# The output projection's first 1024 columns for the forgetting heads as seven block products, issued among the second half of the stick-breaking heads

## The chip, the cores and the metric

The kernel runs on one core of one Trainium2 chip. The metric is the time on the device in microseconds; smaller is better. Three runs of the kernel before took 1096.7 to 1097.93 us, with a median of 1096.99 us.

## What is computed

One layer on 256 tokens of width 2048, in float32. Eight forgetting heads (softmax with a cumulative forget gate) and eight stick-breaking heads, each 128 wide, read one projection of the normed input. Their outputs are normed by group, and one output matrix brings them back:

```python
merged = jnp.concatenate([rms_norm(from_heads(out_a), out_norm_fox_l),
                          rms_norm(from_heads(out_b), out_norm_sb_l)], axis=-1)
return merged @ w_out_l
...
x = x + hybrid_mixer(h, ...)
h = rms_norm(x, ffn_norm[layer])
x = x + conv_ffn(h, w_up[layer], conv_w[layer], conv_b[layer], w_down[layer])
```

`merged @ w_out` is 256 x 2048 times 2048 x 2048. Its first 1024 rows belong to the forgetting heads and the last 1024 to the stick-breaking heads. The change concerns the forgetting heads' rows.

## The kernel before, in words

**Matmuls.** A float32 operand is kept as a rounded high part and a low rest, and a product is made of three matmuls per block of 128 rows: high x high, low x high, high x low. A block of weights of 128 x 2048 numbers (1 MB) is loaded by a DMA of SP's queue into `w_raw` (three buffers). Then it is split (`split`): ACT rounds it into `w_hi` (L231) and DVE subtracts for `w_lo` (L234), with two buffers each. `in_three` (L248 to L259) issues the matmuls with the activations as the stationary operand (L256); `feature_major` issues those with the weights stationary (L282, L288).

**Seven products.** `in_seven` (L609) multiplies a 2 x 2 block matrix of activations (two tiles of 128 tokens, two groups of four heads) by a 2 x 2 block matrix of weights (four 128-row blocks by 512 columns each) with seven block products in place of eight. A block product is 12 matmuls of 512 columns in one PSUM bank. Some take sums of activation blocks (`block_sums`, then the parts of them) and sums of weight blocks: the first is `w_sum` plus `x12` on DVE (L628), the later ones are accumulating DMAs of POOL's queue (L618). After each product DVE adds the bank to the rows of x, scaled (`residual`, L986). It is a generator: each `next` issues one product.

**Stick-breaking heads.** `sb_head` (L923) is a generator of three parts, and `step` advances two heads at a time, so heads 4 and 5 go together, then 6 and 7. Part one is the scores `ps_z` on PE (L925, L562). ACT and DVE then work on them: three activations (L931 to L933), `sp` (L938), a minimum with the mask (L939), a scan `after` (L941), `e` = scores minus scan (L944), an exponential on ACT (L945), and a second minimum with the mask (L947). Part two is the transposes of `e` into `ps_p` on PE (L811), which ACT copies to `w` and `w1` (L814, L815) and DVE completes (L816). Part three is the product with the values, `ps_o` (L795, L796). ACT takes it out (L396), DVE makes the low part (L397), and ACT squares it (L404).

**Order of the work.** The order on PE is the order in which the code issues. On DVE and ACT it is made by a scheduler when the program is built, and each of these engines then takes its instructions strictly in that order. In the stick-breaking half the code does four pairs of `feature_major` products (queries and keys of four heads), then the values (`project`). Then come, for the forgetting rows of `w_out`, columns 0 to 511 and 512 to 1023 as plain products (`token_major`, 48 matmuls each), with heads 4 to 7 stepped between, and then columns 1024 to 2047 in seven products between the plain products of the stick-breaking rows. After each 512 finished columns `next_rows` transposes x for the next stage: two times four transposes `ps_x` (L149), taken out by ACT (L154) and DVE (L157).

**PSUM.** Each of the pools `psa`, `psb` and `pss` has two buffers. The seven products' `bank_a` and `bank_c` lie in `pss` and `bank_b` in `psb`. The `ps_x` tiles lie in `psb`, the `ps_z` and `ps_p` tiles in `pss`, and `ps_o` in `psb`.

Of the kernel before, what the change touches and what calls it, by code (L numbers as in the profile page):

```python
# [9 lines left out]
F32 = mybir.dt.float32  # L10
# [5 lines left out]
P = 128  # L16
D = 2048
# [29 lines left out]
def hybrid_layer(  # L47
# [251 lines left out]
    def feature_major(w, c0, pool, tag):  # L299

        acc = pool.tile([P, 2, 512], F32, name="pu", tag=tag)
        for kh in range(2):
            from_features(acc, weights(rows_of(w, 8 * kh, 8, c0, 2 * P), 8, 2 * P, 16), kh, low_first=kh == 1)
            step()
        return acc
# [9 lines left out]
    with ExitStack() as actx:  # L315
# [264 lines left out]

        def block_sums(parts):

            blocks = [
                at.tile([P, 4, S], F32, name=f"blocks{h}", tag=tag) for h, tag in enumerate(("minus_c1", "blocks"))
# [17 lines left out]

        def in_seven(src, of_tile, sums, w, x12, add, places, idle_steps, prepared, at_once, cols=512, halfway=None):
# [8 lines left out]
            def of_sums(h, t):  # L612
                return lambda i, part, _: sums[part][:, 4 * h + i, t * P : (t + 1) * P]
# [20 lines left out]
            def product(bank, lhs, parts, to, minus=False):  # L634
                new = bank not in banks
                if new:
                    pool, tag = places[bank]
                    banks[bank] = pool.tile([P, 512], F32, name=bank, tag=tag)[:, :cols]
# [14 lines left out]
            product("bank_a", of_blocks(0, 0), prepared(lambda: split(w, 4, cols), sum_weights), (0, 0))  # L653
            if not at_once:
                yield
                first_loads(moved_x12, (w12,))
# [33 lines left out]
        def values_in_seven():  # L690
# [11 lines left out]
            def prepared(split_first, sum_weights):  # L702
# [5 lines left out]
                lambda i: hT[i], [sums[:, part] for part in range(2)],  # L708
# [80 lines left out]
        def weighted(v, hs, w):  # L789
# [3 lines left out]
            po = psb.tile([P, S], F32, name="ps_o", tag="t")  # L793
# [76 lines left out]
        def sb_heads(c0, scale, parts):  # L870
# [3 lines left out]
            for i in range(0, 4, 2):  # L874
                acc = feature_major(wi, c0 + i * P, psa, "acc")
# [15 lines left out]
        def sb_queries(half):  # L891
# [10 lines left out]
            return sb_heads(B0 + 512 * half, QSCALE, parts)  # L902

        def sb_keys(half):
# [9 lines left out]
            return sb_heads(B0 + WF + 512 * half, 1.0, parts)  # L914
# [6 lines left out]
        def sb_head(h, qT, kT, v):  # L921
            (q0, *q), (k0, *k) = qT[h % 4], kT[h % 4]
# [31 lines left out]
            attended(weighted(v, slice((h % 4) * HD, (h % 4 + 1) * HD), (w, w1)), h, g_sb, 1)  # L954

        for half in range(2):
            qT = sb_queries(half)
            if half:
                fox_sums = block_sums([oT_fox[0][:, 4 * i : 4 * i + 4] for i in range(2)])
            kT = sb_keys(half)  # L960
            v = []
            earlier = list(heads)
            for h in range(4 * half, 4 * half + 4):
                heads.append(sb_head(h, qT, kT, v))
            acc = project(B0 + 2 * WF + 512 * half, 512)

            assert not half or not any(g in heads for g in earlier)
# [4 lines left out]
            values(v, acc)  # L972

# [10 lines left out]
        def residual(t, c, ps, factor):  # L984
            xs = xt[t][:, c : c + 512]
            dve.scalar_tensor_tensor(xs, ps, factor[:, t : t + 1], xs, op0=ALU.mult, op1=ALU.add)  # L986

        def out_in_seven(c0, plus_rg, minus_rg):

            def prepared(split_first, sum_weights):  # L990
                with tc.issue_after(last_head[0].ins), tc.issue_after(last_head[1].ins):
                    parts = split_first()
                    sum_weights()
                    sums.extend(big.tile([P, NH, S], F32R, name="oT_sums", tag=f"hT{g}") for g in (1, 2))
                    block_parts(fox_sums, sums)
                return parts

            def add(t, h, ps, minus=False):
                residual(t, c0 + 512 * h, ps, minus_rg if minus else plus_rg)

            sums = []
            return in_seven(
                [rows_of(wo, 4 * h, 4, c0 + 512 * i, 512) for h in range(2) for i in range(2)],
                lambda i: oT[i], sums, at.tile([P, 2048], F32, name="w_sum", tag="vA"),
                [big.tile([P, 2048], F32, name="x12", tag="hT0")], add,
                {"bank_a": (pss, "s"), "bank_b": (psb, "t"), "bank_c": (pss, "s")}, 3, prepared, True,
            )

        rgs = [const.tile([P, NT], F32, name=f"rg{group}") for group in range(2)]
        minus_rg = const.tile([P, NT], F32, name="minus_rg")  # L1010
        seven = out_in_seven(1024, rgs[0], minus_rg)

        ordered[0] = True
        for group, rg in enumerate(rgs):
            if group == 1:
                finish()
            for c in range(4 if group else 2):
                acc = token_major(
                    lambda k: oT[group * NH + k], wo, group * NH, NH, 512 * c, 512,
                    seven,  # L1020
                )
                if group == c == 0:
                    assert scored[: NH + 4] == list(range(NH + 4))
# [389 lines left out]
```

## Time and profile before

| | |
|---|---|
| median of three runs | 1096.99 us |
| span of the profiled execution | 1094.7 us |
| PE busy | 1089.0 us (99%), 5844 matmuls |
| DVE busy | 907.0 us (83%) |
| ACT busy | 721.8 us (66%) |
| POOL busy | 52.8 us (5%) |
| DMA | 251.15 MB, mean 229 GB/s |

The span is one execution from its first to its last instruction, and it lies 2.3 us under the median of the runs. A row of a group of instructions tells the line, the engine, the operation, output<-inputs by tile name, the shape and the count; then busy time and the mean time of one. A row of the timeline or of the chain tells the start, the time it took, and what ran. In the chain a matmul's time is its share of the pipeline, in the timeline it is the matmul's own time from start to end. PE is TensorE, DVE VectorE, ACT ScalarE, POOL GpSimd, SP the queue that issues most loads.

### The profile page before, as it was taken

What the parts mean: (1) busy time and instruction counts of PE and PEld (TensorE: products, weight loads), DVE (VectorE), ACT (ScalarE), POOL (GpSimd) and SP (SyncE); (2) the same over time, 40 slices, a digit from 0 to 9 for tenths busy, and PEclk for the clock granted to TensorE, in tenths of its full rate; (3) what the DMA queues carried; (4) which work ended last, traced back from release to release, by engine and by line L of the source; (5) the groups of instructions that cost most, each with busy time, mean ns of one, the idle gap of its engine ahead of it and who ended that gap; (6) DMA issues with size and microseconds to landing.
All of it is one profiled execution on the core that took longest, in us unless ns stands there. A gap on an engine that the chain in (4) does not pass through costs nothing.

```text
span 1094.7 us, 14881 instructions
## 1 busy us (share of the span) xinstructions
PE 1089.0 (99%) x5844; PEld 944.8 (86%) x5844; DVE 907.0 (83%) x972; ACT 721.8 (66%) x929; POOL 52.8 (5%) x52
## 2 busy tenths in 40 slices
PE   9999999999999999999999999999999999999998
PEld 7998888888888888888888888888888888888887
DVE  5867878877789776789889988889798889889896
ACT  6756555764665567767767776677676777667753
POOL 0011000000000000001010000100000010100010
PEclk9999999999999999999999999999999999999999
DMA  8697654676639395558999697977979698987985
GB/s 290 228 264 212 215 154 154 195 236 203 214 121 286 114 330 192 178 182 229 281 233 282 193 262 264 258 259 184 324 203 308 206 228 271 258 267 190 323 212 173
DMA packets 182575, 251.15 MB, mean 229 GB/s; under 512 B 4528, under 2 KB 120650, under 8 KB 182250
## 3 DMA queue, kind: packets, MB, share of 16 engines
q1 hardware_dynamic: 162474, 209.67, 58.0%
q0 software_dynamic: 19712, 40.01, 19.7%
q8 instruction: 46, 0.75, 0.3%
q10 hardware_dynamic: 320, 0.53, 0.2%
q14 instruction: 23, 0.19, 0.0%
HBM read 248.08 MB, written 2.11 MB: 229 GB/s over the span
## 4 chain that ended last, share of the span: by engine, by line
PE 99%; DMA 0%; DVE 0%; SPq 0%; issue 0%
PE pu L282 35%; PE acc L256 19%; PE pu L288 18%; PE bank_a L256 12%; PE bank_b L256 6%; PE bank_c L256 3%; PE acc L468 2%; PE acc L1291 1%; PE ps_x L149 1%; PE ps_o L795 1%; PE bank_a L1291 1%; PE ps_p L811 0%; DMA w_raw<-in_w_in_dram 0%; PE ps_o L796 0%; PE ps_h L335 0%; PE ps_s L562 0%
## 5 line engine op out<-in xcount | busy, mean ns | idle before, releaser
L234 DVE TENSOR_TENSOR w_lo<-w_raw,w_hi 128x2048 fp32r<-128x2048 f32 (+1 forms) x192 | 431.8, 2252 | 104.1 <-ACT w_hi L231 103.8
L231 ACT CAST w_hi<-w_raw 128x2048 fp32r<-128x2048 f32 (+1 forms) x192 | 360.9, 1882 | 208.8 <-PE pu L282 58.5
L282 PE MATMUL pu<-hT,w_hi 128*128 128x512 f32 x1664 | 393.9, 390 | 0.0
L282 PEld LDWEIGHTS pu<-hT,w_hi 128*128 128x128 f32 x1664 | 310.4, 188 | 62.9
L288 PEld LDWEIGHTS pu<-hT,w_lo 128*128 128x128 f32 x1664 | 209.0, 189 | 6.8
L288 PE MATMUL pu<-hT,w_lo 128*128 128x256 f32 x1664 | 212.2, 282 | 0.0
L256 PE MATMUL acc<-w_hi,hT 128*128 128x512 f32 (+1 forms) x512 | 113.5, 374 | 0.0
L256 PEld LDWEIGHTS acc<-w_hi,hT 128*128 128x128 f32 x512 | 91.5, 188 | 14.2
L234 DVE TENSOR_TENSOR w_lo<-w_sum,w_hi 128x2048 fp32r<-128x2048 f32 (+1 forms) x38 | 84.2, 2215 | 20.4 <-ACT w_hi L231 20.3
L231 ACT CAST w_hi<-w_sum 128x2048 fp32r<-128x2048 f32 (+1 forms) x38 | 70.3, 1851 | 45.3 <-PE pu L282 35.1
L1108 ACT ACTIVATE tap<-up,ccol 128x256 f32<-128x256 f32 x176 | 74.6, 495 | 0.0
L256 PE MATMUL acc<-w_lo,hT 128*128 128x512 f32 (+1 forms) x256 | 58.9, 372 | 0.0
L1213 POOL DMA_DIRECT2D w_sum<-in_w_down_dram x20 | 25.7, 1283 | 674.6 <-DVE w_lo L234 660.3
L256 PEld LDWEIGHTS acc<-w_lo,hT 128*128 128x128 f32 x256 | 46.4, 188 | 7.5
L256 PE MATMUL bank_a<-w_hi,g 128*128 128x512 f32 x160 | 40.0, 393 | 0.0
L256 PE MATMUL bank_a<-w_hi,s 128*128 128x512 f32 x160 | 40.0, 392 | 0.0
L256 PE MATMUL bank_b<-w_hi,s 128*128 128x512 f32 x160 | 40.0, 392 | 0.0
L256 PEld LDWEIGHTS bank_a<-w_hi,g 128*128 128x128 f32 x160 | 28.9, 189 | 5.3
L256 PEld LDWEIGHTS bank_a<-w_hi,s 128*128 128x128 f32 x160 | 28.9, 189 | 5.2
L256 PEld LDWEIGHTS bank_b<-w_hi,s 128*128 128x128 f32 x160 | 28.9, 189 | 5.2
L1113 DVE TENSOR_TENSOR gate<-gate,tap 128x512 f32<-128x512 f32 x44 | 30.3, 689 | 2.5 <-ACT tap L1108 0.2
L1113 DVE TENSOR_TENSOR val<-val,tap 128x512 f32<-128x512 f32 x44 | 30.3, 689 | 2.3
(282 smaller groups left out, 1165.9 us busy)
## 6 DMA issues: line engine op xcount, KB each, us to landing
w_raw<-in_w_up_dram SPq DMA_DIRECT2D x88, 1024.0 KB, 7.2
w_raw<-in_w_down_dram SPq DMA_DIRECT2D x44, 1024.0 KB, 7.5
w_raw<-in_w_in_dram SPq DMA_DIRECT2D x36, 1024.0 KB, 5.6
w_sum<-in_w_down_dram POOLq DMA_DIRECT2D x20, 1024.0 KB, 9.6
w_raw<-in_w_out_dram SPq DMA_DIRECT2D x14, 1024.0 KB, 5.3
w_raw<-in_w_down_dram POOLq DMA_DIRECT2D x10, 1024.0 KB, 14.7
w_raw<-in_w_in_dram SPq DMA_DIRECT2D x10, 688.0 KB, 4.3
w_raw<-in_w_in_dram SPq DMA_DIRECT2D x6, 512.0 KB, 6.9
```

Source lines behind the costliest of these rows:

```text
L149: nc.tensor.transpose(ps[:, j, t * P : (t + 1) * P], xt[t][:, (k + j) * P : (k + j + 1) * P], ident)
L231: copied = act.copy(hi[:, some], r[:, :m])
L234: rest = dve.tensor_tensor(lo[:, some], r[:, :m], f32(hi[:, some]), op=ALU.subtract)
L256: nc.tensor.matmul(o, lhs(i, l, t), r[:, i, :], start=starts and j == 0, stop=stops and j == 3 * n - 1, skip_group_check=more,)
L282: nc.tensor.matmul(acc[:, j, :], hi[:, i, j * P : (j + 1) * P], hT[k].rearrange("p a b -> p (a b)"), start=k == 0, stop=low_first and k == ...
L288: nc.tensor.matmul(acc[:, j, S:], lo[:, i, j * P : (j + 1) * P], hT[k][:, 0, :], start=False, stop=not low_first and k == KT - 1,)
L468: nc.tensor.matmul(acc[:, t, :], of_half(hT[2 * c + i + j], l, t), r[:, j, :], start=high and c == i == m == 0, stop=not high and c == 7 a ...
L795: nc.tensor.matmul(po, v[j][:, hs], wp[:, k], start=i == 0, stop=False)
L1108: act.activation(taps[w][:, j, :], u[:, j, w : w + S], AF.Copy, scale=ccol[:, w, f : f + 1])
L1113: dve.tensor_tensor(a, a, tap, op=ALU.add)
L1213: nc.gpsimd.dma_start(mem[into][:, : nk * 512].rearrange("p (a b) -> p a b", a=nk), src, accum_op=ALU.add)
L1291: nc.tensor.matmul(o, of_half(g, l, t), r[:, i, c0 : c0 + cols], start=kh == 0 and j == 0, stop=kh == n - 1 and j == 11,)
```

## The change

The forgetting rows of columns 0 to 1023 become a second set of seven products, `first_seven`; those of columns 1024 to 2047 stay in seven, as `second_seven`. The block sums and their parts are made once, earlier, and serve both. Until x is loaded for the residual, the upper half of x's buffer holds two temporary tiles: first the rounded sums, then the weight sum's second operand (`x12`, in two halves). So x is loaded again in two parts (`load_again`).

The second stick-breaking half is put in another order: queries and keys of heads 4 and 5, then the values, then queries and keys of heads 6 and 7. Products of `first_seven` are issued between the pieces of the values and of those queries and keys. Heads 4 and 5 are stepped under the values. Heads 6 and 7 are stepped under two pieces of the stick-breaking rows, the end of `first_seven` and the start of `second_seven`. `ps_o` of heads 4 to 7 moves to `pss`; `bank_a` and `bank_c` move to `psb`, and `bank_b` takes over `bank_c`'s bank.

The core of the diff:

```diff
+                if new and places[bank] in banks:
+                    banks[bank] = banks[places[bank]]
+                elif new:
...
+        def block_parts_in_place(blocks, between, lows):
+
+            for hi, block in zip(between, blocks):
+                in_order(act.copy(hi, block))
+            for h, (hi, block) in enumerate(zip(between, blocks)):
+                for i, n, lo in lows[h]:
+                    in_order(dve.tensor_tensor(lo, block[:, i : i + n], f32(hi[:, i : i + n]), op=ALU.subtract))
+            highs = [at.tile([P, 4, S], F32R, name=f"sum_high{h}", tag=tag) for h, tag in enumerate(BLOCKS)]
+            for high, hi in zip(highs, between):
+                in_order(act.copy(high, f32(hi)))
+            return highs
...
+                {"bank_a": (psb, "t"), "bank_c": (psb, "t"), "bank_b": "bank_c"}, idle_steps, prepared, True,
...
+        qT = queries((0,))
+        fox_blocks = block_sums([oT_fox[0][:, 4 * i : 4 * i + 4] for i in range(2)])
+        group_factors(0)
...
+        kT = keys((0,))
...
+        load_again(0)
...
+        first_seven = out_in_seven(
+            0, at.tile([P, 2048], F32, name="w_sum", tag="vA"), spare, 1, prepared_first
+        )
+        next(first_seven)
...
+        v1, ready = [], []
+        add_heads(4, qT, kT, ready, (pss, "s"))
+        sb_values(1, v1, some_of(".777"))
+        qT = queries((2,), behind=some_of("7."))
+        kT = keys((2,), behind=some_of("7."))
+        ready.extend(v1)
...
+        accs = [new_acc()]
+        out_piece(accs[0], 0, 0)
+        step()
+        next(first_seven)
+        add_heads(6, qT, kT, ready, (pss, "s"))
+        step()
+        assert not next(first_seven, None)
+        load_again(1)
+        accs.append(new_acc())
+        out_piece(accs[1], 1, 0)
+        step()
+        second_seven = out_in_seven(1024, ...)
+        next(second_seven)
+        step()
+        next(second_seven)
+        next(second_seven)
+        finish()
+        next(second_seven)
+        out_piece(accs[0], 0, 4)
+        group_factors(1)
+        completed(0, accs[0])
+        out_piece(accs[1], 1, 4)
+        completed(1, accs[1])
+        waiting.append(next_rows(0))
+        for c in range(2, 4):
+            acc = new_acc()
+            for k in (0, 4):
+                next(second_seven, None)
+                out_piece(acc, c, k)
+                step()
...
```

In the built program PE has 3524 matmuls of 512 columns where it had 3536, and its other matmuls are as before. DVE gets two more operations of 2048 columns, three of 1024 and five of 512 columns. ACT gets two more casts of 2048 and four of 1024 columns. From the first weights of the up-projection on, the order on all engines is as before. Three places show what the new order does; each row has its own kernel's line numbers.

**DVE, heads 4 and 5, from a scan to the second head's masked `e`.** `w_lo` is a weight block's low part, `w<-ps_p` needs the transposes of the head that comes first. Before:

```order
L941 SCALAR_TENSOR_TENSOR after<-go_on,sp 128x384
L944 TENSOR_TENSOR e<-ps_z,after 128x384
L938 SCALAR_TENSOR_TENSOR sp<-ps_z,e 128x384
L947 TENSOR_TENSOR e<-e,masks 128x2x128
L939 TENSOR_TENSOR sp<-sp,masks 128x2x128
L941 SCALAR_TENSOR_TENSOR after<-go_on,sp 128x384
L944 TENSOR_TENSOR e<-ps_z,after 128x384
L234 TENSOR_TENSOR w_lo<-w_raw,w_hi 128x2048
L947 TENSOR_TENSOR e<-e,masks 128x2x128
L234 TENSOR_TENSOR w_lo<-w_raw,w_hi 128x2048
L816 TENSOR_TENSOR w<-ps_p,w 128x256 x2
```

Now:

```order
L956 TENSOR_TENSOR sp<-sp,masks 128x2x128
L987 SCALAR_TENSOR_TENSOR x_2428<-bank_a,rg_1556,x_2428 128x512
L958 SCALAR_TENSOR_TENSOR after<-go_on,sp 128x384
L961 TENSOR_TENSOR e<-ps_z,after 128x384
L234 TENSOR_TENSOR w_lo<-w_raw,w_hi 128x2048
L964 TENSOR_TENSOR e<-e,masks 128x2x128
L955 SCALAR_TENSOR_TENSOR sp<-ps_z,e 128x384
L956 TENSOR_TENSOR sp<-sp,masks 128x2x128
L958 SCALAR_TENSOR_TENSOR after<-go_on,sp 128x384
L833 TENSOR_TENSOR w<-ps_p,w 128x256
L961 TENSOR_TENSOR e<-ps_z,after 128x384
L964 TENSOR_TENSOR e<-e,masks 128x2x128
```

Before, both heads' masked `e` stood ahead of both `w<-ps_p`. Now the first head's `w<-ps_p` stands ahead of the second head's `e` and its mask. On PE the two heads' transposes still follow one another directly.

**DVE, heads 6 and 7, up to the second head's masked `e`.** Before:

```order
L938 SCALAR_TENSOR_TENSOR sp<-ps_z,e 128x384
L405 TENSOR_TENSOR ssq_103<-ssq_103,osq 128x256
L939 TENSOR_TENSOR sp<-sp,masks 128x2x128
L941 SCALAR_TENSOR_TENSOR after<-go_on,sp 128x384
L944 TENSOR_TENSOR e<-ps_z,after 128x384
L938 SCALAR_TENSOR_TENSOR sp<-ps_z,e 128x384
L939 TENSOR_TENSOR sp<-sp,masks 128x2x128
L941 SCALAR_TENSOR_TENSOR after<-go_on,sp 128x384
L944 TENSOR_TENSOR e<-ps_z,after 128x384
L234 TENSOR_TENSOR w_lo<-w_raw,w_hi 128x2048
L947 TENSOR_TENSOR e<-e,masks 128x2x128 x2
```

Now, from the second head's `sp` on:

```order
L955 SCALAR_TENSOR_TENSOR sp<-ps_z,e 128x384
L234 TENSOR_TENSOR w_lo<-w_sum,w_hi 128x2048
L964 TENSOR_TENSOR e<-e,masks 128x2x128
L956 TENSOR_TENSOR sp<-sp,masks 128x2x128
L643 TENSOR_TENSOR w_sum<-w_sum,x_3173 128x2048
L234 TENSOR_TENSOR w_lo<-w_raw,w_hi 128x2048
L234 TENSOR_TENSOR w_lo<-w_sum,w_hi 128x2048
L958 SCALAR_TENSOR_TENSOR after<-go_on,sp 128x384
L987 SCALAR_TENSOR_TENSOR x_2428<-bank_a,rg_1556,x_2428 128x512
L961 TENSOR_TENSOR e<-ps_z,after 128x384
L833 TENSOR_TENSOR w<-ps_p,w 128x256
L964 TENSOR_TENSOR e<-e,masks 128x2x128
```

One operation of 2048 columns stood among the second head's; now there are four.

**PE, where `bank_b` starts.** Before, from the first product in seven on:

```order
L256 MATMUL bank_a<-w_hi,oT_fox 128x512 x8
L256 MATMUL bank_a<-w_lo,oT_fox 128x512 x4
L256 MATMUL bank_c<-w_hi,oT_fox 128x512 x8
L256 MATMUL bank_c<-w_lo,oT_fox 128x512 x4
L256 MATMUL acc<-w_hi,oT_2305 128x512 x8
```

Now, in `second_seven`, where `bank_b` has `bank_c`'s name and place:

```order
L256 MATMUL bank_a<-w_hi,oT_fox 128x512 x8
L256 MATMUL bank_a<-w_lo,oT_fox 128x512 x4
L828 MATMUL ps_p<-cs,e 128x128 x6
L256 MATMUL bank_c<-w_hi,oT_fox 128x512 x8
L256 MATMUL bank_c<-w_lo,oT_fox 128x512 x4
L256 MATMUL bank_c<-w_hi,sum_high_2565 128x512
```

The transposes of heads 6 and 7 stand between `bank_a` and `bank_c`, and `bank_b`'s first product follows `bank_c`'s directly in the same bank, where 24 matmuls stood between.

More of the change, by code (lines that the diff above doesn't have):

```diff
@@ L304, in feature_major @@
             step()
+            next(behind, None)
         return acc
@@ L982, in next_rows @@
             yield
[L984 to L1006, printed above, removed]
-            )
```

166 lines of the change are left out of this document (103 added, 63 removed).

## The prediction

> **What bounds the kernel now.** I read the page first. Its line of busy times has PE at work nearly all the span.
>
> ```profile
> PE 1089.0 (99%) x5844; PEld 944.8 (86%) x5844; DVE 907.0 (83%) x972; ACT 721.8 (66%) x929; POOL 52.8 (5%) x52
> ```
>
> A busy PE need not be a PE at its full pace, so I went on to the chain of waits from 270 to 460 us, the stage of the change. Its columns are start, time and what ran.
>
> ```profile
> 279.86 0.36 PE ps_z L562 x3
> 280.22 10.90 PE acc L256 x48
> 291.12 0.66 PE ps_p L811 x6
> ...
> 326.52 2.72 PE bank_c L256 x12
> ```
>
> The chain there is PE alone, and 48 matmuls of 512 columns in 10.90 us and 12 in 2.72 us are both 0.227 us each: PE runs without a gap, before the seven products and in them. So a matmul less saves 0.227 us, and a wait of PE is lost in full, since nothing later has slack to give it back. The question is how near the other engines are. The timeline of DVE for heads 4 and 5 answers it.
>
> ```profile
> 281.55 0.56 DVE L938 SCALAR_TENSOR_TENSOR sp<-ps_z,e 128x384 f32<-128x384 f32 x1
> 282.14 0.43 DVE L939 TENSOR_TENSOR sp<-sp,masks 128x256 f32<-128x256 f32 x1
> 282.60 0.96 DVE L941 TENSOR_TENSOR_SCAN after<-go_on,sp 128x384 f32<-128x384 f32 x1
> 283.59 0.56 DVE L944 TENSOR_TENSOR e<-ps_z,after 128x384 f32<-128x384 f32 x1
> 284.07 0.55 DVE L938 SCALAR_TENSOR_TENSOR sp<-ps_z,e 128x384 f32<-128x384 f32 x1
> 284.74 0.43 DVE L947 TENSOR_TENSOR e<-e,masks 128x256 f32<-128x256 f32 x1
> 285.08 0.42 DVE L939 TENSOR_TENSOR sp<-sp,masks 128x256 f32<-128x256 f32 x1
> 285.54 0.96 DVE L941 TENSOR_TENSOR_SCAN after<-go_on,sp 128x384 f32<-128x384 f32 x1
> 286.53 0.56 DVE L944 TENSOR_TENSOR e<-ps_z,after 128x384 f32<-128x384 f32 x1
> 287.00 2.28 DVE L234 TENSOR_TENSOR w_lo<-w_raw,w_hi 128x2048 fp32r<-128x2048 f32 x1
> 289.20 0.42 DVE L947 TENSOR_TENSOR e<-e,masks 128x256 f32<-128x256 f32 x1
> ```
>
> The second head's masked `e` is done at 289.62 and PE wants it at 291.12. The margin is 1.5 us: DVE sets no pace, but one split (2.20 from its start to the next row's) more in this piece would.
>
> **The saving.** The first 1024 columns cost two times 48 matmuls and now cost seven times 12. That is 12 fewer, as the counts of the built program say (3536 to 3524), so 12 x 0.227 = 2.7 us. All of it is on the path.
>
> **What DVE is charged.** These rows give the rest of the prices, each from its start to the next where that is shown.
>
> ```profile
> 263.35 0.68 DVE L312 TENSOR_TENSOR t<-pu,t 128x512 f32<-128x512 f32 x1
> 263.95 0.68 DVE L592 TENSOR_TENSOR blocks<-blocks 128x512 f32<-128x512 f32 x1
> ...
> 267.36 0.69 DVE L884 TENSOR_TENSOR k_low<-t,kB 128x512 fp32r<-128x512 f32 x1
> ...
> 321.97 2.29 DVE L628 TENSOR_TENSOR w_sum<-w_sum,x 128x2048 f32<-128x2048 f32 x1
> ...
> 327.17 1.21 DVE L601 TENSOR_TENSOR oT_sums<-blocks,oT_sums 128x1024 fp32r<-128x1024 f32 x1
> 328.30 2.28 DVE L234 TENSOR_TENSOR w_lo<-w_raw,w_hi 128x2048 fp32r<-128x2048 f32 x1
> 334.51 0.74 DVE L986 SCALAR_TENSOR_TENSOR x<-bank_a,rg,x 128x512 f32<-128x512 f32 x1
> ```
>
> A 512-column operation is 0.6, a sum or low part of 1024 columns 1.13, a sum of 2048 columns 2.2 like a split, a residual 0.7. DVE has 2 x 2.2 + 3 x 1.13 + 3 x 0.7 + 2 x 0.6 = 11 us more to do. Spread over the 190 us of that chain, it would fit into its idle time (17% by the page). It isn't spread: the order puts it ahead of what PE waits for. ACT's extra casts are off the path, except as named under C.
>
> **A, the transposes of head 4.** I start at the moment when `k_low` of heads 4 and 5 is ready, which their scores need. From the sum `t` to the end of `k_low` took 4.7 us before (263.35 to 268.05); with ACT's copy ahead of it and four short operations put in, it is near 7, about what PE has from there (`ps_o`, 24 matmuls), so the two come level. From here DVE must do, before head 4's masked `e`: two `ssq` (0.34 each), `sum_low` in three pieces (1.13 + 2 x 0.6), four splits (8.8), the weight sum in two halves (2.26), and head 4's `sp`, minimum, scan, `e` and mask with a residual between (0.5 + 0.46 + 0.99 + 0.48 + 0.42 + 0.7). Sum 17.6. PE has the rest of `ps_z` (0.8) and 60 matmuls (13.6), 14.4. It waits 3.2. If DVE had kept the 1.5 us of margin, 1.7. More, if the weight sum also waits for `x12`:
>
> ```profile
> w_raw<-in_w_in_dram SPq DMA_DIRECT2D x10, 688.0 KB, 4.3
> ```
>
> `x12` takes the place of the rounded sums, so its load goes out only when ACT has copied them. At some 4.3 us for the nearest size, less one split and a piece that DVE does meanwhile, that adds 1.5: the upper end is 4.7.
>
> **B, the transposes of head 5.** This is a closed loop of the new order. PE's transposes of head 4, then ACT's copy, then DVE's `w<-ps_p` of head 4, only then head 5's `e`, its exponential on ACT, its mask, and PE again. The ACT rows:
>
> ```profile
> 287.12 0.53 ACT L945 ACTIVATE e<-e 128x384 f32<-128x384 f32 x1 [0.61 <-DVE e L944]
> ...
> 291.48 0.37 ACT L814 CAST w<-ps_p 128x256 fp32r<-128x256 f32 x1 [0.24 <-PE ps_p L811]
> ...
> 306.49 0.38 ACT L404 ACTIVATE osq<-ps_o 128x256 f32<-128x256 f32 x1
> ...
> 327.47 0.65 ACT L404 ACTIVATE osq<-ps_o 128x256 f32<-128x256 f32 x2
> ```
>
> After head 4's mask DVE has `sp`, minimum and scan of head 5 (1.95, in which PE's three transposes and ACT's copy fit), `w<-ps_p` 0.34, `e` 0.56, the exponential 0.53, the mask 0.42: 3.8, less the 0.33 of the transposes, is 3.5. Were DVE early at A, the first 1.95 would be done, and 0.37 + 0.34 + 0.56 + 0.53 + 0.42 = 2.2 would stay, 2.3 with handovers. It can't be less.
>
> **C, the scores of heads 6 and 7.** `ps_o` of heads 4 and 5 now lies in `pss`, so `ps_z` waits until ACT has squared it. Between the two squares ACT has a cast (1.8). These are the ends of `ps_o` before:
>
> ```profile
> 303.65 0.22 PE ps_o L796 x2
> ...
> 323.55 0.22 PE ps_o L796 x2
> ```
>
> To the last square it took 3.0 us there (303.87 to 306.87) and 4.35 (323.77 to 328.12). PE has 12 matmuls and one head's scores between, 3.3. So 3.0 + 1.8 - 3.3 = 1.5; 0 if the cast falls into ACT's idle time, 2.9 by the slower case.
>
> **D, the transposes of head 7.** From the end of `ps_z` to the second head's `sp` took 3.85 (280.22 to 284.07), at least the 2.5 between the two `sp`, and 4.5 with the residual that stands there now. Then DVE does `sp` 0.5, three splits 6.6, mask and minimum 0.7, the weight sum 2.2, scan 0.99, residual 0.7, `e` 0.56, exponential 0.53, mask 0.42: 13.2. PE has 48 matmuls and three transposes, 11.2. It waits 3.85 + 13.2 - 11.2 = 5.8, between 4.5 and 6.5.
>
> **E and F, PSUM.** For E, `bank_b` can't start before DVE has read `bank_c`. For F, the two `ps_x` tiles of the first `next_rows` share one buffer of `psb`, since `bank_a` of `second_seven` holds the other. The rows, of the chain and then of DVE:
>
> ```profile
> 342.85 2.72 PE bank_b L256 x12
> ...
> 367.84 0.87 PE ps_x L149 x8
> ```
>
> ```profile
> 345.60 0.75 DVE L986 SCALAR_TENSOR_TENSOR x<-bank_b,rg,x 128x512 f32<-128x512 f32 x1 [0.30 <-PE bank_b L256]
> ...
> 368.04 2.29 DVE L234 TENSOR_TENSOR w_lo<-w_raw,w_hi 128x2048 fp32r<-128x2048 f32 x1 [1.87 <-ACT w_hi L231]
> 370.25 1.66 DVE L157 SCALAR_TENSOR_TENSOR hT<-ps_x,pcol,hT 128x256 fp32r<-128x256 f32 x4
> ```
>
> E: the bank ends at 345.57 and the residual at 346.35, so 0.8, taken as 0.9; a second use of the bank may add 1. F: the first tile is read at 371.1, half way through the four, where PE wanted the second at 368.3, so 2.8; without the split ahead 1.8; up to 3.3 if a residual stands there too.
>
> **The sum.** 3.2 + 3.5 + 1.5 + 5.8 + 0.9 + 2.8 = 17.7, less 2.7: 15.0 us. The profiled span of 1094.7 becomes 1109.7, and the median, which is 2.3 above the span, becomes 1112.0. All low ends give 1.7 + 2.3 + 0 + 4.5 + 0.8 + 1.8 - 2.7 = 8.4 (1105.4), all high ones 4.7 + 3.5 + 2.9 + 6.5 + 1.9 + 3.3 - 2.7 = 20.1 (1117.1).
>
> POOL gets accumulating transfers for `first_seven` and x's load in two parts. I cost them at nothing: in the order each lands several pieces of PE work ahead of its reader. If one came late, it would lengthen the waits named.
>
> **The rivals.**
>
> *No waits.* DVE is idle 17% of the span, more than its extra 11 us in the reordered stage. If it ran ahead far enough, PE would keep its pace: 1096.99 - 2.7 = 1094.3, faster. The place is the same DVE queue, and the point is a lead of 3.2 us at `k_low`. Against it: a lead can't open loop B, which PE's own transposes start. Chance 0.04.
>
> *Only the closed loops.* DVE has lead enough for A and C: B 2.3, D 4.5, E 0.8, F 1.8, less 2.7, gives +6.7, 1103.7. The margin of 1.5 speaks against that much lead. Chance 0.12.
>
> *PE slow after long waits.* PE's first matmuls, after idling, ran at half pace; 16 of the same width later took 1.89. The first row is of the timeline, the second of the chain:
>
> ```profile
> 1.06 3.12 PE L421 MATMUL idle<-zeros 128*128 128x256 bf16 x14 [1.06 <-DVE zeros L411]
> ```
>
> ```profile
> 405.69 1.89 PE pu L288 x16
> ```
>
> That is 0.22 against 0.118 each, 1.5 us lost in 3.12. If A with B (6.7 together) and D (5.8) each bring this back, it is 3.0 more: 1115.0. For it, the waits are long; against it, they are broken by three transposes, and no row here shows a wait of such length in mid-run. Chance 0.20. [...]
>
> That the change does not do what it says is out: the counts and the order show it.
>
> **How the numbers follow.** The forecast has 0.62, the rivals 0.04, 0.12 and 0.20, and 0.02 is left for a result near zero. The time is 1112.0. The range reaches from the closed loops alone (1103.7) to the clock case with most of the high ends (20.1 + 3.0 gives 1120.1): 1104 to 1120. About 0.2% (2.2 us) is what a measurement can tell here from no change: faster 0.04, same 0.02, slower 0.94.
>
> **What would show it.** In the profile after, the chain should leave PE for DVE at the transposes of heads 4 to 7, with PE idle before `ps_p` about 3, 3.5 and 6 us, before `bank_b` 1 and before the second `ps_x` 3. If PE's pace stays at 0.227 us through these places, I am wrong about the order's weight; if matmuls after a wait take 0.43 us each, the clock case holds.

## The result and the profile after

The changed kernel takes 1121.21 us (median of four runs, 1118.9 to 1122.6) where the kernel before takes 1096.94 in the same measurement (1096.7 to 1097.93): a ratio of 1.0217, with a 95% interval of 1.0204 to 1.0229. It is slower by 24.3 us. The forecast was slower by 15.0, and its range ended at 1120, 1.2 us below the median.

The busy times on the page of after, to be held against the first line that the prediction shows:

```profile
PE 1096.3 (98%) x5832; PEld 948.0 (85%) x5832; DVE 917.2 (82%) x982; ACT 728.7 (65%) x935; POOL 59.0 (5%) x58
```

PE has 12 matmuls fewer and is busy 7.3 us longer (1096.3 to 1089.0), and the span grew by 25.7 (1120.4 to 1094.7). So there are two losses: PE waits, and what it does takes longer. They separate in the stage from the last transposes of the first half's heads to those of `pcc` in the up-projection, which the windows give as one row for before and one for after; the columns are window, length, then the busy time of PE, PEld, DVE, ACT and POOL, then the granted clock, the DMA share and GB/s.

```profile
243.71:407.42 163.71, 163.60 (x838) 139.43 (x837) 129.67 (x151) 95.63 (x125) 3.90 (x3) 1.00 0.67 207
```

```profile
244.56:433.36 188.80, 169.85 (x823) 142.19 (x822) 139.31 (x158) 102.05 (x129) 10.03 (x9) 0.94 0.71 202
```

The stage is 25.1 us longer. PE idles 18.95 us in it where it idled 0.1, and it is busy 6.25 us more. The mean granted clock fell from 1.00 to 0.94. The idle time is in the list of PE's waits from 240 to 440 us (waiter, what released it, us in total, times, longest); before, that list was empty.

```profile
PE ps_p L828 <- DVE e L964: 13.3, 3, 6.4
PE ps_x L149 <- DVE hT L157: 3.0, 1, 3.0
PE ps_z L942 <- ACT osq L405: 1.8, 2, 1.2
PE bank_c L256 <- DVE x L987: 0.8, 1, 0.8
```

These are A, B and D (first row), F, C and E of the prediction, and no other; in E's row `bank_b` goes by the name of `bank_c`, whose tile it uses. The timeline of PE has each with the work behind it; the bracket is the idle time and its releaser.

```profile
276.47 0.87 PE L828 MATMUL ps_p<-cs,e 128*128 128x128 f32 x3 [4.12 <-DVE e L964]
280.18 0.87 PE L828 MATMUL ps_p<-cs,e 128*128 128x128 f32 x3 [2.84 <-DVE e L964]
280.71 3.76 PE L256 MATMUL bank_c<-w_hi,oT_fox 128*128 128x512 f32 x8
284.27 1.55 PE L256 MATMUL bank_c<-w_lo,oT_fox 128*128 128x512 f32 x4
...
345.27 0.49 PE L828 MATMUL ps_p<-cs,e 128*128 128x128 f32 x3
352.12 0.87 PE L828 MATMUL ps_p<-cs,e 128*128 128x128 f32 x3 [6.36 <-DVE e L964]
...
388.57 1.08 PE L149 MATMUL ps_x<-cs,x 128*128 128x128 f32 x4 [3.00 <-DVE hT L157]
```

The eight first matmuls of the product behind A and B take 3.76 us, 0.45 each from start to start where the prediction reads 0.227, and three transposes take 0.87 where three of the same take 0.49. That is half pace. I laid windows of 3.41 us along the steps in which the granted clock changes (it stands ahead of the DMA share):

```profile
271.60:275.01 3.41, 0.75 (x4) 0.28 (x2) 3.38 (x5) 1.41 (x2) 0.00 (x0) 1.00 1.07 302
275.01:278.42 3.41, 0.87 (x3) 0.50 (x3) 3.34 (x6) 0.54 (x2) 0.00 (x0) 0.50 1.08 271
278.42:281.84 3.42, 1.66 (x6) 1.49 (x7) 1.20 (x4) 1.06 (x3) 0.00 (x0) 0.50 1.07 382
281.84:285.25 3.41, 3.41 (x10) 2.64 (x9) 0.25 (x1) 0.69 (x1) 0.00 (x0) 0.50 0.30 93
...
329.62:333.04 3.42, 2.30 (x12) 1.48 (x10) 3.01 (x5) 1.86 (x2) 0.00 (x0) 1.00 1.03 401
...
346.69:350.10 3.41, 0.00 (x0) 0.00 (x0) 3.41 (x4) 0.34 (x2) 0.81 (x1) 1.00 0.89 136
350.10:353.52 3.42, 1.40 (x5) 1.34 (x6) 1.61 (x4) 1.02 (x3) 0.49 (x1) 0.50 1.09 249
353.52:356.93 3.41, 3.41 (x9) 2.64 (x9) 0.42 (x1) 0.49 (x2) 0.00 (x0) 0.50 1.08 279
...
384.24:387.65 3.41, 1.33 (x8) 0.89 (x7) 2.31 (x2) 1.91 (x3) 0.00 (x0) 1.00 0.06 23
387.65:391.06 3.41, 2.49 (x8) 2.23 (x9) 1.27 (x4) 0.84 (x2) 0.00 (x0) 0.50 0.00 0
391.06:394.48 3.42, 3.42 (x9) 2.64 (x9) 0.38 (x1) 1.38 (x1) 0.00 (x0) 0.50 0.00 0
```

The chain of waits has the twelve products behind D as one piece (start, time, what ran), 4.65 us where twelve took 2.72:

```profile
352.99 4.65 PE bank_c L256 x12
```

A window in which PE had 0.75 us of work is followed by a granted clock of 0.50, and in this run the clock comes back only behind a window that is full (3.41 or 3.42 us). This happens behind A with B (the first four rows), behind D and behind F (the last two groups). It did not happen at C, where PE was busy 2.30 us of a window.

### The profile page after: what moved, and what is told of

The parts are those of the page before. It is cut to its first block, busy times and chain, and to the rows that moved or that the text cites. A ratio compares the mean times of both kernels' runs of the same rounds, so it can differ in the third digit from the quotient of the medians.

```text
span 1120.4 us, 14907 instructions
## 1 busy us (share of the span) xinstructions
PE 1096.3 (98%) x5832; PEld 948.0 (85%) x5832; DVE 917.2 (82%) x982; ACT 728.7 (65%) x935; POOL 59.0 (5%) x58
## 4 chain that ended last, share of the span: by engine, by line
PE 68%; issue 3%; DMA 1%; DVE 1%; ACT 1%; ACTq 0%; POOLq 0%
PE pu L282 29%; PE pu L288 15%; PE bank_a L256 11%; PE bank_b L256 5%; PE bank_c L256 3%; PE acc L256 3%; PE acc L1387 1%; DMA w_sum<-in_w_out_dram 1%; DVE w_lo L234 1%; ACT w_hi L231 1%; PE bank_a L1387 1%; PE ps_x L149 0%; DVE w_sum L643 0%; DVE hT L157 0%; PE ps_p L828 0%
## 5 line engine op out<-in xcount | busy, mean ns | idle before, releaser
L234 DVE TENSOR_TENSOR w_lo<-w_raw,w_hi 128x2048 fp32r<-128x2048 f32 (+1 forms) x190 | 427.2, 2252 | 105.0 <-ACT w_hi L231 104.8
L231 ACT CAST w_hi<-w_raw 128x2048 fp32r<-128x2048 f32 (+1 forms) x190 | 357.1, 1882 | 215.3 <-PE pu L282 61.4
L231 ACT CAST w_hi<-w_sum 128x2048 fp32r<-128x2048 f32 (+1 forms) x42 | 77.8, 1854 | 52.8 <-PE pu L282 35.0
L234 DVE TENSOR_TENSOR w_lo<-w_sum,w_hi 128x2048 fp32r<-128x2048 f32 (+1 forms) x42 | 93.3, 2222 | 19.3 <-ACT w_hi L231 19.3
L1309 POOL DMA_DIRECT2D w_sum<-in_w_down_dram x20 | 25.7, 1284 | 676.8 <-DVE w_lo L234 676.8
```

The lines of the kernel that those rows point to most:

```text
L231: copied = act.copy(hi[:, some], r[:, :m])
L234: rest = dve.tensor_tensor(lo[:, some], r[:, :m], f32(hi[:, some]), op=ALU.subtract)
L1309: nc.gpsimd.dma_start(mem[into][:, : nk * 512].rearrange("p (a b) -> p a b", a=nk), src, accum_op=ALU.add)
```

## The experiments

The theory: PE waits because of the order in DVE's queue (A, B, D), of ACT and DVE steps that stand behind splits (C), and of shared PSUM places (E, F); and these waits take the clock to half behind them. The first rival: the half pace has another cause, or the waits alone explain the time. The second: the load of DVE in this stage counts, not its order. Ratios are to the kernel before.

**1. Filling the waits, in the tile of the transposes.** In `transposed_weights`, and ahead of the second `ps_x`:

```diff
+        def keep_warm(tile, n):
+            for _ in range(n):
+                nc.tensor.matmul(tile, zeros[:, :P], zeros, start=True, stop=True)
...
+            keep_warm(pt[:, 0:2, :].rearrange("p a b -> p (a b)"), warm)
             for i in range(3):
                 nc.tensor.transpose(pt[:, i, :], e[:, i, :], ident)
...
+                if k == 2:
+                    keep_warm(pss.tile([P, S], F32, name="warm", tag="s"), 20)
```

> The changed kernel, with small matmuls on zeros put on PE ahead of the transposes of heads 4, 5 and 7 (30, 18 and 48 of 256 columns, into the tile that the transposes then overwrite) and 20 ahead of the second ps_x, so that PE works through about three quarters of its waits; DVE, ACT and the transfers keep their order. Theory (the waits A to F stay as long as they are, 18.9 us in the profile of after, and the half pace behind them is the rest, 10.0 us): the granted clock shows no half-rate stretch in 265 to 400 us, the products behind the waits take 2.72 us again, and the time falls by 8 to 10 us, to 1111 to 1113. Rival 1 (the half pace comes of the place, not of PE's idleness): the half-rate stretches stay and the time stays within 2 us of 1121. Rival 2 (the waits would be shorter at a full clock, since PE is part of the loop): the time falls by more than 10.

Measured: 1124.01 us, ratio 1.0243 (1.0228 to 1.0259). Neither the theory nor a rival holds: the time rose by 2.8. The reason is the experiment's own. The filling did not start when PE ran dry, since the tile takes the place of `ps_z`, which DVE still reads:

```profile
349.51 7.54 PE L826 MATMUL ps_p<-zeros 128*128 128x256 bf16 x48 [5.25 <-DVE e L966]
```

PE idled 5.25 us at D, the granted clock was 0.50 from 347.08 to 353.90 us, and PE worked through the 48 empty matmuls at half pace for part of the way. The masked `e` was ready at 350.47, and the transposes started at 356.89. At A, B and F the filling left waits of 1.42, 1.27 and 0.81 us, and no half pace stands behind them (granted clock 1.00); but as the filling itself delayed PE, the time of this run does not price the clock.

**2. The heads' steps first.**

```diff
+            with tc.high_priority(offset=2 * AHEAD) if h >= 4 else nullcontext():
                 e = tmp.tile([P, 3, P], F32, name="e", tag="pr")
...
                 dve.tensor_tensor(diagonal, diagonal, limit2, op=ALU.min)
```

> The changed kernel, with the ACT and DVE steps of heads 4 to 7 from Abs to the masked e put ahead of the weight splits in the order; the second head's mask then stands ahead of both w<-ps_p, and only the splits that stand between are behind it. Nothing is left out. Theory (DVE's order makes A, B and D, 13.3 us of waiting, and they bring two of the three half-rate stretches): the waits before ps_p fall to under 3 us together, no half-rate stretch stands behind them, and F with its stretch stays: 1121 less 10 to 13 less about 5 to 6, so 1103 to 1107. Rival (DVE has too much work in this stage, whatever its order): the wait moves from the transposes to the matmuls that need w_lo, PE is idle as long as before and the time stays above 1115.

Measured: 1112.54 us, ratio 1.0141 (1.0124 to 1.0158), four runs from 1109.84 to 1114.58. The list of PE's waits:

```profile
PE ps_p L828 <- DVE e L965: 6.7, 2, 4.5
PE ps_x L149 <- DVE hT L157: 3.0, 1, 3.0
PE ps_z L942 <- ACT osq L405: 2.3, 2, 1.6
PE bank_c L256 <- DVE x L988: 0.8, 1, 0.8
```

The 13.3 us before the transposes became 6.7, in two waits: loop B is open (the second head's mask stands ahead of both `w<-ps_p`), A is halved to 2.2, D fell to 4.5. So order alone was worth 8.7 us of the time. The time lies between the theory (1103 to 1107) and the rival (above 1115): the theory asked for more, but the weight sums and `bank_c`'s split still stood ahead of the second mask.

**3. The second pair of `ps_x` one piece later.**

```diff
             for k in range(4 * c, 4 * c + 4, 2):
                 transposed_split(k, g_ffn)
+                if k == 0:
+                    yield
```

> The changed kernel, with the second pair of the first ps_x tiles one piece of work later, behind the next 12 products and 24 matmuls; the order is otherwise the same. Theory (F is a wait for a PSUM buffer, 3.0 us, and brings the third half-rate stretch, 2.8 us): no wait before ps_x, no half-rate stretch at 385 to 395 us, the time falls by 5 to 6 us, to 1115 to 1116. Rival (the wait is for DVE, which is late anyway): the wait stands before the next bank_a product or the next ps_x instead, and the time falls by less than 2.

Measured: 1115.85 us, ratio 1.0173 (1.0157 to 1.0188), 5.4 less than the change. In its profile no wait stands before `ps_x`, and the granted clock is 1.00 from 356 us on. F cost 3.0 as a wait; the other 2.4 fit the half pace behind it, which is gone too. The theory holds here in both parts.

**4. Both edits.** The built kernel has one thing more than the expectation names: the steps at the end of heads 4 and 5 (the scaled output, its low part, the square and its sum) are put ahead in the order too.

> The changed kernel with both edits: the heads' steps ahead of the splits, and the second pair of ps_x one piece later. Theory: A, B, D and F gone but for 3 us, no half-rate stretch, C 1.8 and E 0.8 left, 12 matmuls fewer (2.7): 1097 + 3 + 2.6 - 2.7, about 1100, between 1097 and 1103. Rival (DVE's work itself is too much, or the late accumulating transfers are the cause): above 1110.

Measured: 1108.03 us, ratio 1.0099 (1.0082 to 1.0116). It lies between the two expectations. PE still waits 2.15 for the transposes of heads 4 and 5, 4.99 before those of head 7, 1.97 at C and 0.84 at E, and behind D the granted clock is 0.50 once more, from 344.81 to 348.22 us. The third edit did not shorten C, which was 1.78 in the changed kernel.

**5. Filling the waits, in the open accumulator.** Zeros added to the sum that PE is in the middle of need no buffer:

```diff
+    def keep_warm(n):
+        for _ in range(n):
+            nc.tensor.matmul(
+                now_open[0][:, 0, :256], idle_zeros[0][:, :P], idle_zeros[0], start=False, stop=False,
+                skip_group_check=True,
+            )
```

> The changed kernel, with PE's waits filled once more, now by matmuls on zeros that add nothing to the accumulator which is open at that place, so that they need no buffer of their own: 30 of 256 columns ahead of the transposes of head 4, 18 of head 5, 46 of head 7 and 20 ahead of the second ps_x. By the first filled run one takes about 0.117 us, so 3.5, 2.1, 5.4 and 2.3 us of waits of 4.1, 2.8, 6.4 and 3.0. Theory (half pace follows PE's idleness): no half-rate stretch, the products behind take 2.72 us, the ends of the waits stay where DVE puts them: 8 to 10 us less, 1111 to 1113. Rival (filling doesn't help, DVE is what counts and the half pace hides in its delays): within 2 us of 1121.

Measured: 1115.21 us, ratio 1.0168 (1.0154 to 1.0183), 6.0 less than the change. Place D in the timeline of PE:

```profile
344.94 0.49 PE L840 MATMUL ps_p<-cs,e 128*128 128x128 f32 x3
345.26 5.18 PE L218 MATMUL acc<-zeros 128*128 128x256 bf16 x46
351.65 0.52 PE L840 MATMUL ps_p<-cs,e 128*128 128x128 f32 x3 [1.20 <-DVE e L976]
```

The transposes of head 7 still start 6.4 us after the wait's beginning, so DVE alone sets that. But they take 0.52 where they took 0.87, and no stretch at half pace is left at A, B, D and F (granted clock 1.00). It is less than the theory asked, and the profiled execution shows why: B is 0.5 longer (PE is sooner where it waits for DVE), C is 2.4 instead of 1.8, and a step at half pace is new at C (0.50 from 331.70 to 335.11 us). That execution is the slowest of the four, 1117.04 us; the others took 1114.98 to 1115.22 at a mean clock of 0.999 to 1.000, so most of them seem to be without this step. PE did nothing useful more and the kernel is 6.0 us faster: at A, B, D and F the half pace went when PE's idleness was filled.

**6. The sums and `bank_c`'s split behind the masks.** On top of the edits of runs 2 and 3, without the third one of run 4 (only the sums of `first_seven` are shown here; those of `second_seven` are gated alike):

```diff
             parts = split_first()
-            sum_weights()
+            with tc.issue_after(masked[-1].ins):
+                sum_weights()
...
-                if here == "7":
+                if here == "m":
+                    last_split.append(masked[-1])
+                if here != ".":
                     next(first_seven)
...
-        next(second_seven)
+        with tc.issue_after(masked[-1].ins):
+            next(second_seven)
```

> The kernel of the last run with both edits, and more of DVE's order: the weight sums of both seven products, and the splits for bank_c, stand behind the second head's masked e, since nothing needs them before. Theory (order alone makes A and D; 2.2 and 5.0 us are left of them in the profile of the kernel with both edits): ps_p waits under 1 us together, a wait before bank_b of 1 to 2.5 may stand in their place, C 2.0 stays: 1098 to 1101. Rival (DVE's load in this stage is what PE waits for, in whatever order): what is moved behind the mask is missing later, PE waits before bank_c and bank_b as long as before ps_p, and the time stays at 1106 or above.

Measured: 1105.23 us, ratio 1.0077 (1.0061 to 1.0093). In its profile no transposes wait any more, and the granted clock is 1.00 all through the stage. This execution is the fastest of the four, 1104.02 us; the others have mean clocks of 0.997 to 0.998 and are 0.7 to 2.4 us longer, so their clock seems to have fallen somewhere. Two waits took the place of those at the transposes, in the first two rows:

```profile
PE bank_c L256 <- DVE x L990: 2.8, 1, 2.8
PE bank_c L256 <- ACT w_hi L231: 2.2, 1, 2.2
PE ps_z L944 <- ACT osq L405: 2.0, 2, 1.6
PE pu L282 <- ACT w_hi L231: 0.8, 1, 0.8
```

The first is a residual behind two splits, before the second `bank_b` product. The second is the weight sum, now too late for `bank_b`. Of 7.1 us of A and D some 5.0 came back elsewhere. Both sides are partly right: order makes the waits at the transposes, and DVE is full enough here that most of what is put first is missing later.

**7. C and E too.** On top of run 6, the splits and casts behind the heads' low parts and squares, and `bank_b` of `second_seven` in `bank_a`'s place. In this kernel `bank_b` overwrites the first product of `bank_a`, to which later products add, so that part of the sums is lost.

```diff
-                {"bank_a": (psb, "t"), "bank_c": (psb, "t"), "bank_b": "bank_c"}, idle_steps, prepared, True,
+                {"bank_a": (psb, "t"), "bank_c": (psb, "t"), "bank_b": again}, idle_steps, prepared, True,
...
+        low_after, cast_after = squared
+        with tc.issue_after(low_after.ins):
             assert not next(first_seven, None)
...
+        with tc.issue_after(cast_after.ins):
             out_piece(accs[1], 1, 0)
```

> The same, with C and E too: the splits and casts that stood between the heads' low parts and squares stand behind them, and bank_b of second_seven takes bank_a's place, which is free by then. Theory: of A to F nothing is left but 1 to 2 us, the 12 matmuls fewer (2.7 us) show: 1095 to 1097, at or below the kernel before. Rival (the late accumulating transfers, or ACT, hold PE in another place): no faster than the run without these two edits, 1098 or above.

Measured: 1106.46 us, ratio 1.0078 (1.0065 to 1.0092). It is no faster than run 6, as the rival said. The scores no longer wait, but a `bank_a` product right behind them waits 1.25 for a residual; the wait for the weight sum grew to 3.0, that for the later residual is 3.0, and behind both of these the granted clock is now 0.50 for a step (from 341.88 to 345.29 and from 352.12 to 355.53 us). What C gave was lost there.

**8. The new order, with plain products in `first_seven`'s places.**

```diff
-        first_seven = out_in_seven(0, ...)
+        first_seven = out_plain(0)
...
+            for i in range(2):
+                banks = [psb.tile([P, 512], F32, name=f"bank{i}{t}", tag="t") for t in range(NT)]
+                for h in range(2):
+                    parts = weights(rows_of(wo, 4 * h, 4, c0 + 512 * i, 512), 4, 512)
+                    in_three(
+                        banks, parts, 4, lambda k, part, t: of_half(oT[4 * h + k], part, t), h == 0, h == 1
+                    )
...
```

> The changed order, with the first 1024 columns as plain products (8 pieces of 12 matmuls from 4 weight blocks, with no weight sums and no accumulating transfers) at the places of first_seven; second_seven as in the change. It tells the reordering from the seven products. Theory (the seven products' DVE work, three splits of 2.2 and the sums, is what makes A, B and most of D): A and B gone, D about 1, C 0 to 1, E 0.8 and F 3.0 with 0 to 2.8 of half pace stay, nothing saved: 1102 to 1106. Rival (the reordering itself makes the waits): above 1112.

Measured: 1110.24 us, ratio 1.0118 (1.0104 to 1.0133). It lies between the theory (1102 to 1106) and the rival (above 1112). A, B and D are gone altogether, as the theory says of the seven products' DVE work; their accumulating transfers are gone too, but in runs 2 and 6 they were there, and order alone shortened or removed these waits. C grew to 4.8 us in one wait, since no product stands between `ps_o` and `ps_z` in this kernel, and the granted clock is 0.50 for 6.8 us from within it (328.03 to 334.85); F is 3.0, E 1.3. So it tells where A, B and D come from. How much the reordering costs by itself it doesn't tell, because its own pieces lie differently at C.

**9 and 10. One wait alone, in the kernel before.** On head 5, ahead of its mask, eight and sixteen times:

```diff
             act.activation(flat, flat, AF.Exp)
+            for _ in range(8 if h == 5 else 0):
+                dve.tensor_tensor(flat, flat, flat, op=ALU.max)
             diagonal = e[:, 0::2, :]
```

> The kernel before, with nothing of the change; only on DVE eight operations that leave head 5's e as it is (the maximum of e with itself, 384 columns, some 0.47 us each) ahead of its mask. In the order one weight split and head 4's w<-ps_p get in between, so the masked e comes at about 295.9 us where it came at 289.6, and PE waits about 4.7 us between the transposes of heads 4 and 5, where it never waited. It prices one wait by itself. Theory (a wait of this length takes PE's clock to half for one or two grid steps of 3.41 us behind it): the wait plus 1.7 to 3.4, 1103.4 to 1105.2. Rival (the half pace in the changed kernel has another cause, such as the load of its transfers): the wait alone, 1101.7, and a granted clock of 1.00 all through.

> The same with sixteen such operations: the masked e at about 299.7, a wait of about 8.4 us. Theory: the clock falls within the wait and comes back a grid step after the matmuls do, so the half pace costs about as much as behind the shorter wait, 1.7 to 3.4: 1107.1 to 1108.9. Rival (half pace grows with the length of the wait): 1110 or above. Rival (no half pace): 1105.4.

Measured: 1104.24 us, ratio 1.0068 (1.0051 to 1.0085), and 1109.25 us, ratio 1.0116 (1.0101 to 1.0131), both against 1096.43. The timeline of PE, first with eight, then with sixteen:

```profile
296.80 0.88 PE L811 MATMUL ps_p<-cs,e 128*128 128x128 f32 x3 [5.34 <-DVE e L949]
297.33 6.29 PE L256 MATMUL acc<-w_hi,hT 128*128 128x512 f32 x16
```

```profile
302.66 0.87 PE L811 MATMUL ps_p<-cs,e 128*128 128x128 f32 x3 [10.09 <-DVE e L949]
303.19 5.54 PE L256 MATMUL acc<-w_hi,hT 128*128 128x512 f32 x16
```

From start to start the 16 products take 6.13 (to 303.46) and 5.38 (to 308.57) where 16 x 0.227 is 3.63. So half pace costs 2.5 and 1.75 there, and the transposes 0.4 each. Wait and half pace make 8.2 and 12.2 us; measured are 7.8 and 12.8. The first is within the theory's 1103.4 to 1105.2. The second lies between the theory (to 1108.9) and the rival of a growing half pace (from 1110), because its wait came out at 10.09 where 8.4 was expected; the half pace itself, 2.1 with the transposes, did not grow. The granted clock was 0.50 from 295.62 to 302.44 us with eight and from 296.43 to 306.67 with sixteen. Nothing of the change is in these kernels: the wait of 5.34 us cost 2.5 us beyond its length, and the one of 10.09 us cost 2.7 beyond it.

**11. Most of the waits.** On top of run 6, the squares and low parts as in run 7 (without the bank), and the residuals of the seven products ahead of splits:

```diff
+                with tc.high_priority(offset=2 * AHEAD):
                     residual(t, c0 + 512 * h, ps, minus_rg if minus else rgs[0])
```

> The gated kernel of before (heads' steps first, ps_x apart, weight sums and bank_c's split behind the masks), with the squares of heads 4 and 5 and their low parts ahead of the splits and casts that delayed them, and the residuals of both seven products ahead of splits. Its profile showed C 2.05, a wait of 2.17 before bank_b for the weight sum, 2.81 before the second bank_b product for a residual that stood behind two splits, and 0.77 before pu. Theory (order can still move the residual; the weight sum is load): C and the 2.81 go, 2.2 to 3 stay: 1105.2 less 4 to 5, 1100 to 1101.5. Rival (DVE is full in this stage, so what is put ahead is paid by what stands behind): within 1.5 of 1105.

Measured: 1102.35 us, ratio 1.0050 (1.0035 to 1.0065), 2.9 less than run 6, so the rival (within 1.5 of 1105) falls, and 0.9 above what the theory asked. C and the residual's wait are gone. One wait of more than 0.2 us is left:

```profile
PE bank_c L256 <- ACT w_hi L231: 3.7, 1, 3.7
```

It is the chain of weight sum and cast ahead of `bank_b`. It ends at 342.88 us where in run 6 it ended at 342.68: PE only came 1.3 us sooner and waits there for what it gained. Behind it the granted clock is 0.50 for one step (window 342.73 to 346.14):

```profile
342.73:346.14 3.41, 3.26 (x8) 2.59 (x9) 3.28 (x2) 1.90 (x2) 0.44 (x1) 0.50 0.84 128
```

So of the 24.3 us that the change cost, 5.9 are left, each against the kernel before of its own measurement. The other 18.4 are a matter of order, of shared places and of the clock behind the waits. No run came below the kernel before.

## Why the prediction was right and wrong

**The direction and the waits** were right. In the stage PE waits at the six places named, and nowhere else, and each wait lies in its range:

| place | forecast | range | measured |
|---|---|---|---|
| A, transposes of head 4 | 3.2 | 1.7 to 4.7 | 4.12 |
| B, transposes of head 5 | 3.5 | 2.3 to 3.5 | 2.84 |
| C, scores of heads 6 and 7 | 1.5 | 0 to 2.9 | 1.78 |
| D, transposes of head 7 | 5.8 | 4.5 to 6.5 | 6.36 |
| E, `bank_b` | 0.9 | 0.8 to 1.9 | 0.84 |
| F, second `ps_x` | 2.8 | 1.8 to 3.3 | 3.00 |
| all | 17.7 | | 18.94 |

The sum is near partly because misses offset each other: A, C, D and F came out longer, B and E shorter. B's 3.5 is its loop at full pace; its 2.84 is the wait left over when the three transposes ahead of it run at half pace (0.87 us). In run 3, where they take 0.52, B is 3.19.

A is nearer to its upper end for the reason that the upper end names. The timeline of DVE has the weight sum waiting for `x12`:

```profile
264.11 1.23 DVE L643 TENSOR_TENSOR w_sum<-w_sum,x 128x1024 f32<-128x1024 f32 x1 [1.37 <-DMA x<-in_w_out_dram]
```

**The saving** of 2.7 us is there only in part. A product of block sums takes 2.80 us where I took 2.72: in the timeline of after, the one at 291.10 ends where the next tile starts, at 293.90. Eight of them take 0.6 back.

**The step that failed** is the term for the clock. The forecast's sum had it at nothing, and the rival that had it priced it too low. "For it, the waits are long; against it, they are broken by three transposes, and no row here shows a wait of such length in mid-run", said the prediction, and gave the case 0.20 and a price of 3.0 us for two returns. The three transposes between A and B are 0.87 us of a window of 3.41 (from 275.01), and the granted clock was still 0.50 in the next one; those of head 6 stand ahead of the whole of D. There were three returns, not two, since one stands behind F with its 3.0 us too. And each cost 2.3 to 3.0 us, not 1.5: 2.2 on `bank_c`'s 12 products and 0.8 on the transposes behind A and B, 1.9 and 0.4 at D, 2.4 and 0.4 at F, about 8.1 in all where the rival had 3.0. The price was taken from the start of the kernel, where PE ran from idle into a continuous stream. Here the first window at half pace is still partly idle (PE busy 0.87, 1.40 and 2.49 us behind A, D and F), and the clock stays at half for a second or third one (to 285.25, 356.93 and 394.48 us). With 18.94 + 8.1 + 0.6 - 2.7 = 24.9 the stage's 25.1 us are accounted for.

With the measured 8 for the clock, the forecast's own terms would have given 1094.7 + 17.7 + 8 - 2.7 + 2.3 = 1120, and all high ends about 1125, beyond the 1121.21 measured. Run 5 fills much of the idleness and comes to 1115.21, nearer to the forecast of 1112.0; runs 9 and 10 show the price without the change.

**Costed at nothing: POOL's transfers.** ACT did wait 1.48 us for `w_sum`'s landing at 326.52, right ahead of C. In run 11 ACT waits for the same landing (1.29 us), and C is gone by order alone. So they lengthen C only through the cast and split that wait for them ahead of the heads' low parts, as the prediction allowed.

**The rivals.** "No waits" fell at once. "Only the closed loops" fell with A at 4.12. That DVE had 17% of idle time over the span was no argument, as the forecast held against the first rival: in run 6 DVE has idle times of 0.7 and 0.6 us, and no longer one, from 322 to 352 us. What stays open is whether a further order of DVE would come below the kernel before. Run 11 is 5.9 us above it. Its waits (4.4 us) and its step of half pace (1.6, as the product in it takes 4.37 us instead of 2.80), less the saving of 2.7, make only 3.3. Of the other 2.6 the slower products of block sums explain some 0.6; the rest is not explained, so no run shows the saving in full.

## What to carry to other kernels

A wait of PE had two prices here: its length, and what the clock took behind it, 3.0 us at A with B, 2.3 at D, 2.8 at F and none at C. The wait alone did not tell the second: F took the clock to half in the changed kernel (3.00 us, 1.33 us of work in the window of 3.41) and not in run 2 (2.99 us, 2.35 and 1.49 us of work in its two windows). So read the granted clock behind each wait, and count the windows at half clock that are partly idle too. In a queue of fixed order such as DVE's, work that is needed late but ready early belongs behind the short chain that the bottleneck waits for (8.7 us in run 2); but where the queue is full, moving it moves the wait (in run 6 some 5.0 of 7.1 us came back elsewhere).

## What the runs showed of the hardware

In the stage the granted clock changed only on a grid of 3.41 us: in the profile of after at 275.01, 285.25, 350.10, 356.93, 387.65 and 394.48 us, which lie 3, 19, 2, 9 and 2 such steps apart. In the profiles of the changed kernel and of the eleven runs, between 255 and 400 us, every window at full clock with PE busy 1.44 us or less (15 of them, from 0.00 up) was followed by one at half, and none with 1.49 us or more. The nearest two, of runs 8 and 2:

```profile
324.61:328.03 3.42, 1.44 (x12) 1.20 (x10) 0.60 (x2) 2.31 (x3) 0.00 (x0) 1.00 0.81 249
328.03:331.44 3.41, 0.63 (x3) 0.63 (x4) 3.41 (x4) 1.10 (x3) 0.00 (x0) 0.50 0.16 62
```

```profile
373.54:376.95 3.41, 2.35 (x13) 1.75 (x11) 1.46 (x2) 2.75 (x3) 0.00 (x0) 1.00 0.35 133
376.95:380.37 3.42, 1.49 (x9) 1.33 (x10) 1.79 (x3) 0.82 (x2) 0.00 (x0) 1.00 0.00 0
```

So a wait did not have to fill a window; in these profiles PE worked 42% of the fullest window at full clock that half clock followed, and 44% of the emptiest that it did not follow. On the way back, a window at half clock with PE busy 2.49 us (after, at 387.65) was followed by another at half, and one with 2.72 (run 4, at 344.81) by one at 1.00.

The second pair of rows is F in run 2: the same wait of 2.99 us as in the changed kernel, but cut in two by the grid, and without half pace. That fits the scatter of the kernels with such waits, though only one execution of each was profiled: the runs of the changed kernel spread over 3.7 us, with mean clocks of 0.989 to 0.994 and the fastest at 0.994, and those of run 2 over 4.7 us, where the kernel before spreads over 1.2.
